# Encoder block on one core: another order of loads, norm sums and head rotations ahead of attention

## The chip, the core and the metric

The kernel runs on one core of a Trainium2 chip. The core has a matrix engine (PE, with its weight load shown apart as PEld), a vector engine (DVE), a scalar engine (ACT), a general engine (POOL), and a queue of its own for transfers (SP, "SPq" in the rows). The metric is the device time of one execution in microseconds (us); less is better.

## The reference

One layer of an encoder over 1024 tokens of width 1024, in float32:

```
mod = silu(c) @ ada_w + ada_b                    # six vectors of 1024: sh1, sc1, g1, sh2, sc2, g2
h   = rmsnorm(x, norm1_w) * (1 + sc1) + sh1
proj = h @ w_in                                  # q 512 | k 128 | v 128 | z 1024 | xbc 1536 | dt 32 | gates 2048
q, k = axial_rope(rmsnorm(q, q_gain)), axial_rope(rmsnorm(k, k_gain))      # per head of 64
att  = softmax(q k^T / 8) v                      # 8 heads, 2 key/value heads
ssd  = rmsnorm((scan forward + scan backward) * silu(z))                   # state space branch on conv(xbc)
x    = x + g1 * ((gate0 * (att @ w_attn_up) + gate1 * (ssd @ w_ssd_up)) @ w_out)
h2   = rmsnorm(x, norm2_w) * (1 + sc2) + sh2
x    = x + g2 * peer(h2)                         # 8 heads, top 16 of 16384 experts per head
out  = rmsnorm(x, final_norm_w)
```

Only the lines down to `q, k` are touched by the change.

## The kernel before

Everything is held transposed: features stand on the 128 partitions, tokens run along the free axis, so `x` is eight parts of 128 x 1024. Products keep float32 precision by splitting both operands into a high and a low half; `mm3` (L203 to L207) issues three matmuls of 128x512 for each pair, high-high, high-low, low-high. A half is made by `split`: ACT rounds to the high half (L175), another engine subtracts (L176). `w_in` is cut into 43 output tiles of 128; one tile is 8 parts x 2 token halves x 3 = 48 matmuls. `weights` loads a tile in two pieces (`wr`), casts them on ACT (`wh`) and subtracts on POOL (`wl`); each of these names has 3 or 4 buffers.

Two stages matter here.

**First norm (pool `p0`, to L309).** `shift_scale(m)` forms one column each of shift and scale: 128 rows of `ada_w` are loaded (`at`), multiplied by silu(c) with a running sum on DVE (L254), the bias is added (L255), and the scale is joined with the norm's weight (L271). Beside that, ACT squares the eight parts of `x` (L282), PE sums the squares over partitions (`sums`, L212), `rstd` takes the reciprocal root on DVE and ACT with two Newton steps (L218 to L224), PE spreads the result over partitions (`rbcast`, L233) and ACT copies it out (`rb`, L293). Then each part of `x` is multiplied by `rb` (L296), scaled and shifted on ACT (L299), split into `hh` and `hl`, and taken at once into three output tiles, `FIRST = (4, 0, 1)`: keys, and the first two query tiles. The order in DVE, POOL and ACT is that of the code (`manual`).

**Heads (pool `pr`, to L404).** Five tiles hold keys (4) and queries (0 to 3), two heads in each; further tiles made in this stage are values (5) and two gate tiles. For each of the five: `norms` squares the tile, sums over each head's 64 partitions and calls `rstd`; `heads` spreads it (`rbcast`), multiplies with gain (L358), swaps halves of 32 partitions (L360), multiplies by sine on DVE (L362) and by cosine on POOL (L361), adds (L363) and writes high halves (ACT, L368 to L376) and low halves (DVE, L369 to L378). In this stage a scheduler of the program's builder sets the order within each engine. After it comes attention, whose first work on DVE is the row maximum (L450), interleaved with the convolution tiles of the state space branch on PE.

The later stages take the same instructions in both kernels, and each engine has them in the same order from the second of the 16 attention steps on.

Of the kernel before, what the change touches and what calls it, by code (L numbers as in the profile page):

```python
# [20 lines left out]
D = 1024  # L21
# [48 lines left out]
K_BSEL, K_QSEL, N_KN, K_HSEL, K_U, K_L, K_GT, K_LT, N_KB = 0, 32, 544, 544, 1568, 1696, 1824, 1952, 2080  # L70
# [10 lines left out]
def constants():  # L81
# [6 lines left out]
    ka[p, K_FOLD + p % 64] = 1.0  # L88
    kb = np.zeros((128, N_KB), np.float32)
    kb[p, K_BSEL + p // 64] = 1.0  # L90
# [3 lines left out]
    for i in range(4):  # L94
        for s in range(2):
            kb[32 * i + s, K_QSEL + 128 * i + 64 * s:K_QSEL + 128 * i + 64 * s + 64] = 1.0
# [7 lines left out]
    return {"ka": ka, "kb": kb, "kr": kr}  # L104
# [16 lines left out]
def block(ctx, tc, A, out, dbg=None):  # L121
# [143 lines left out]
    done = manual("DVE", "Pool", "Activation")  # L265
    cs = condition(p0.tile([128, D], F32, name="cs"))

    def shift_scale(m):
        ada(m, m + 1, at_tile, cs)
        ada(8 + m, 9 + m, at_tile, cs)  # L270
        V.scalar_tensor_tensor(A1[:, m:m + 1], mod[:, 8 + m:9 + m], 1.0, cols[:, C_N1 + m:C_N1 + m + 1], op0=OP.add, op1=OP.mult)  # L271
# [12 lines left out]
    raws = [p0.tile([128, 8, 128], F32, name="w3r", bufs=2) for _ in range(2)]  # L284
    for m, raw in zip(FIRST[1:], raws):
        nc.sync.dma_start(raw, A["wi"][m])
# [53 lines left out]
    def norms(m, raw):  # L340
        sq = pr.tile([128, S], F32, name="sq")
        ACT.activation(sq, raw, AF.Square)
        acc = P1()
        sums(sq, acc, S, True, True, kb[:, K_BSEL:K_BSEL + 32])
        return m, raw, rstd(pr, acc, S, 1.0 / 64, 3)
# [9 lines left out]
    def heads(m, raw, r):  # L355
        rb = rbcast(P2(), r, S, kb[:, K_QSEL:K_QSEL + 512])
        g = cols[:, C_KG:C_KG + 1] if m == 4 else cols[:, C_QG:C_QG + 1]
        V.scalar_tensor_tensor(v2(raw), v2(raw), g, rb, op0=OP.mult, op1=OP.mult)  # L358
        sw = pr.tile([128, S], F32, name="sw")
        V.stream_shuffle(sw, raw, list(range(16, 32)) + list(range(16)))  # L360
        POOL.tensor_tensor(raw, raw, cos, op=OP.mult)  # L361
        V.tensor_tensor(sw, sw, sin, op=OP.mult)  # L362
        V.tensor_tensor(raw, raw, sw, op=OP.add)  # L363
        dump("qk", m, raw)
        a, b = raw[0:64], raw[64:128]
        if m < 4:
            e, f = qs[2 * m], qs[2 * m + 1]
            ACT.copy(e[0:64], a)  # L368
# [1408 lines left out]
```

## Time and profile before

| | us |
|---|---|
| median of 3 runs (lowest, highest) | 4008.17 (4002.51, 4011.59) |
| the profiled execution, its own time | 4000.45 |
| its span in the profile | 3998.6 |
| PE busy in the span | 3633.1 (91%) |
| DVE, POOL, ACT busy | 2601.3, 1828.6, 1357.6 |

Shares of busy time are means over stages with different limits. The profile's second part shows PE busy for about 5 and 7 tenths in the first two of 40 slices of 100 us and 9 or more tenths in nearly all that follow, with a granted clock of 0.8 of full speed in the first slice. The rows of this stage are in the section on the rows below.

### The profile page before, as it was taken

The page shows a single profiled execution, that of the slowest core. Times are in us where ns is not written, and L with a number is a line of the kernel's source. Part 1 is how long each engine was busy: PE and PEld are TensorE (multiplying, and loading weights), DVE is VectorE, ACT ScalarE, POOL GpSimd, SP SyncE. Part 2 cuts the span into 40 slices and gives each one's busy share as a digit, 9 for nine tenths or more (in the row PEclk, how much of TensorE's full clock was granted, in tenths as well). Part 3 has the DMA queues.
Part 4 walks back from the last instruction along what each step waited for, and adds up shares of the span by engine and source line. Part 5 has one row for each costly group of instructions (what it writes and reads, how often), then busy time and mean ns, then how long its engine had stood idle before and what let it go on. Part 6 is the DMA issues. An engine that isn't in the chain of part 4 may idle for free. (4 is left out here: it accounts for less than half of the span.)

```text
span 3998.6 us, 61125 instructions
## 1 busy us (share of the span) xinstructions
PE 3633.1 (91%) x22927; PEld 3188.4 (80%) x22927; DVE 2601.3 (65%) x5316; ACT 1357.6 (34%) x2658; POOL 1828.6 (46%) x1529
## 2 busy tenths in 40 slices
PE   5799999998898899998888889699999999999998
PEld 3577777776687889996768789697888999788897
DVE  5688851356673578877785467684457898544556
ACT  4265542223333433332226555322222222222222
POOL 3211113555455557777875466444443444444200
PEclk8899999998899999999999899799999999999999
DMA  5111124323366349897777678888887898888732
GB/s 184 37 47 43 54 89 141 103 92 120 96 219 192 119 135 327 310 320 232 248 256 258 226 265 330 326 297 316 317 317 256 299 293 295 300 312 310 246 115 81
DMA packets 386920, 852.08 MB, mean 213 GB/s; under 512 B 32704, under 2 KB 146880, under 8 KB 383808
## 3 DMA queue, kind: packets, MB, share of 16 engines
q1 hardware_dynamic: 276032, 445.47, 33.1%
q0 software_dynamic: 110592, 402.70, 28.8%
q8 instruction: 180, 2.95, 0.3%
q14 instruction: 116, 0.95, 0.1%
HBM read 739.45 MB, written 108.59 MB: 212 GB/s over the span
## 5 line engine op out<-in xcount | busy, mean ns | idle before, releaser
L205 PE MATMUL hb<-ah,wh 128*128 128x320 f32 x2048 | 653.4, 319 | 25.5 <-ACT a L1369 25.5
L207 PE MATMUL hb<-ah,wl 128*128 128x320 f32 x2048 | 641.0, 313 | 9.6 <-issue 9.6
L206 PE MATMUL hb<-al,wh 128*128 128x320 f32 x2048 | 640.1, 313 | 0.0
L1192 POOL DMA_INDIRECT br<-u,bidx x384 | 373.0, 971 | 364.0 <-DVE br L1224 235.4
L195 POOL TENSOR_TENSOR wl<-wr,wh 128x512 fp32r<-128x512 f32 x269 | 352.5, 1316 | 394.6 <-ACT wh L194 364.6
L205 PE MATMUL pb<-Wh,vh 128*128 128x320 f32 x1536 | 476.8, 317 | 55.6 <-ACT Wh L1599 31.7
L176 POOL TENSOR_TENSOR wl<-wr,wh 128x512 fp32r<-128x512 f32 x170 | 232.1, 1369 | 634.9 <-ACT wh L175 455.6
L1192 POOL DMA_INDIRECT br<-v,ixt x384 | 380.0, 990 | 268.4 <-PE gx L1271 154.1
L206 PE MATMUL pb<-Wl,vh 128*128 128x320 f32 x1536 | 480.6, 313 | 2.1 <-DVE Wl L1602 2.1
L207 PE MATMUL pb<-Wh,vl 128*128 128x320 f32 x1536 | 478.7, 312 | 0.6 <-issue 0.6
L1224 DVE SCALAR_TENSOR_TENSOR br<-br,gx 128x1024 f32<-128x1024 f32 x384 | 454.0, 1215 | 8.0 <-DMA br<-u,bidx 5.4
L205 PEld LDWEIGHTS hb<-ah,wh 128*128 128x128 f32 x2048 | 392.5, 192 | 55.2 <-ACT a L1369 29.9
L207 PEld LDWEIGHTS hb<-ah,wl 128*128 128x128 f32 x2048 | 391.5, 191 | 11.0 <-issue 10.9
L206 PEld LDWEIGHTS hb<-al,wh 128*128 128x128 f32 x2048 | 391.9, 191 | 0.0
L1632 DVE TENSOR_TENSOR acc<-acc,pb 128x320 f32<-128x320 f32 x491 | 230.3, 485 | 231.2 <-PE pb L207 170.6
L175 ACT CAST vh<-vr 128x512 fp32r<-128x512 f32 x256 | 151.8, 619 | 636.2 <-PE pb L206 415.5
L205 PEld LDWEIGHTS pb<-Wh,vh 128*128 128x128 f32 x1536 | 289.7, 190 | 84.1 <-ACT Wh L1599 34.9
L194 ACT CAST wh<-wr 128x512 fp32r<-128x512 f32 x288 | 178.3, 619 | 402.5 <-PE hb L206 144.3
L206 PEld LDWEIGHTS pb<-Wl,vh 128*128 128x128 f32 x1536 | 292.4, 190 | 6.3 <-DVE Wl L1602 4.7
L207 PEld LDWEIGHTS pb<-Wh,vl 128*128 128x128 f32 x1536 | 292.6, 190 | 0.4
L1388 DVE TENSOR_TENSOR quad<-io,rig 128x1024 f32<-128x1024 f32 x160 | 191.6, 1221 | 136.7 <-PE pb L1403 77.1
L176 DVE TENSOR_TENSOR vl<-vr,vh 128x512 fp32r<-128x512 f32 x256 | 198.5, 776 | 80.9 <-ACT vh L175 70.0
(362 smaller groups left out, 8266.9 us busy)
## 6 DMA issues: line engine op xcount, KB each, us to landing
wr<-uT SPq DMA_DIRECT2D x256, 256.0 KB
vr<-v SPq DMA_DIRECT2D x256, 256.0 KB
G_d<-stg SPq DMA_DIRECT2D x20, 2048.0 KB
gt<-G_d SPq DMA_DIRECT2D x42, 960.0 KB
a_d<-a SPq DMA_DIRECT2D x85, 320.0 KB
a<-a_d SPq DMA_DIRECT2D x85, 320.0 KB
wr<-wi SPq DMA_DIRECT2D x82, 256.0 KB
sq<-adaT SPq DMA_DIRECT2D x32, 512.0 KB
```

Of the source, the lines that this page charges most:

```text
L175: ACT.copy(hi, src)
L176: (eng or POOL).tensor_tensor(lo, src, f32(hi), op=OP.subtract)
L194: ACT.copy(h, raw)
L195: late.append(lambda: (eng or POOL).tensor_tensor(w, raw, f32(h), op=OP.subtract))
L205: PE.matmul(o, lhsT=wh, rhs=xh, start=first, stop=False)
L206: PE.matmul(o, lhsT=wh, rhs=xl, start=False, stop=False)
L207: PE.matmul(o, lhsT=wl, rhs=xh, start=False, stop=last)
L1192: POOL.indirect_dma_start(out=r, out_offset=None, in_=A[tab], in_offset=bass.IndirectOffsetOnAxis(ap=idx, axis=0))
L1224: V.scalar_tensor_tensor(v2(r), v2(r), 1.0, hrow[0], op0=OP.mult, op1=OP.mult, accum_out=a[:, s:s + 1])
L1388: V.tensor_tensor(x, iota.unsqueeze(1).unsqueeze(1).to_broadcast([128, 2, 4, 128]), ig[:, 0:2, t:t + 4].unsqueeze(3).to_broadcast([128, 2, ...
L1632: V.tensor_tensor(acc[:, m, js], acc[:, m, js], o, op=OP.add)
```

## The change

In the first norm:
- The parts of `x` are loaded ahead of the rows of `ada_w`; the vector silu(c) is written to PSUM (`csP`) and read from there by the projections' products (L285 of the changed kernel, L254 before).
- The running sums go to `sums1`; bias and norm weight are folded in by one tiny ACT instruction for each column (L290, L294) in place of L255 and L271. The first scale column is formed before `rstd`, the other three of the first four after it.
- The spread `rstd` stays in PSUM (`rb`, two banks); multiplication by it and by the scale is one DVE instruction for each token half (L322). ACT adds the shift alone, and POOL makes the low halves `hl` of the first seven parts (DVE before).
- `FIRST` is two tiles, (4, 0); tile 1 is made in the head stage. PE's order is written by hand here too.

In the head stage:
- The norms are batched: one `rstd` for tiles 4 and 0, one for 1 and 2, one for 3. The selecting matrices for this are wider (constant `kb`, 1572 columns where 544 were loaded here).
- The product with cosine moves from POOL to DVE.
- The order on PE and DVE is written by hand: half tiles of projections on PE stand between the spreads and sums, and each rotation (`rotate`, `highs`, `lows`) has its place among them.

The diff, without the layout of constants and the helper functions that keep their text:

```diff
-    for m in range(2):
-        shift_scale(m)
+    done = manual("DVE", "Pool", "Activation", "PE")
+    FIRST = (4, 0)
     xt = p0.tile([128, 8, S], F32, name="xt")
+    cs = p0.tile([128, D], F32, name="cs")
+    nc.sync.dma_start(cs, A["cv"].to_broadcast([128, D]))
     for m in range(8):
         nc.sync.dma_start(xt[:, m], A["xT"][:, m])
-    FIRST = (4, 0, 1)
+    csP = P2()
+    ACT.activation(csP, v2(cs), AF.Silu)
+    def project(i):
+        at = at_tile()
+        nc.sync.dma_start(at, A["adaT"][i])
+        V.scalar_tensor_tensor(v2(at), v2(at), 1.0, csP, op0=OP.mult, op1=OP.mult, accum_out=sums1[:, i:i + 1])
+    def scale_of(m):
+        project(8 + m)
+        n1 = cols[:, C_N1 + m:C_N1 + m + 1]
+        ACT.activation(A1[:, m:m + 1], sums1[:, 8 + m:9 + m], AF.Identity, bias=pre[:, m:m + 1], scale=n1)
...
+    scale_of(0)
     r = rstd(p0, acc, S, 1.0 / D)
-    W3 = [weights(A["wi"][FIRST[0]], 8)]
-    for raw in raws:
-        W3.append([p0.tile([128, 8, 128], FR, name=n, bufs=2) for n in ("w3h", "w3l")])
-        split(raw, *W3[-1])
-    rb = p0.tile([128, S], F32, name="rb")
-    ACT.copy(v2(rb), rbcast(P2(), r, S))
+    shift_of(0)
+    scale_of(1)
+    shift_of(1)
+    raw = p0.tile([128, 8, 128], F32, name="w3r")
+    nc.sync.dma_start(raw, A["wi"][FIRST[0]])
+    W3 = [[p0.tile([128, 8, 128], FR, name=n) for n in ("w3h", "w3l")]]
+    split(raw, *W3[0])
+    W3.append(weights(A["wi"][FIRST[1]], 8))
+    rb = [P1() for _ in range(2)]
...
     for m in range(8):
-        (POOL if m > 1 else V).tensor_tensor(xt[:, m], xt[:, m], rb, op=OP.mult)
-    for m in range(8):
-        t = xt[:, m]
-        ACT.activation(t, t, AF.Identity, bias=mod[:, m:m + 1], scale=A1[:, m:m + 1])
-        split(t, hh[:, m], hl[:, m], V)
+        x = xt[:, m]
+        for j, o in enumerate(rb):
+            js = slice(512 * j, 512 * j + 512)
+            V.scalar_tensor_tensor(x[:, js], x[:, js], A1[:, m:m + 1], o, op0=OP.mult, op1=OP.mult)
+        if m < 7:
+            ACT.activation(x, x, AF.Identity, bias=mod[:, m:m + 1], scale=1.0)
+            split(x, hh[:, m], hl[:, m])
+        else:
+            ACT.activation(hh[:, m], x, AF.Identity, bias=mod[:, m:m + 1], scale=1.0)
+            V.scalar_tensor_tensor(hl[:, m], x, mod[:, m:m + 1], f32(hh[:, m]), op0=OP.add, op1=OP.subtract)
...
         if m < 6:
-            shift_scale(m + 2)
+            scale_of(m + 2)
+            shift_of(m + 2)
...
-        POOL.tensor_tensor(raw, raw, cos, op=OP.mult)
-        V.tensor_tensor(sw, sw, sin, op=OP.mult)
+            V.tensor_tensor(sw, sw, sin, op=OP.mult)
+            V.tensor_tensor(raw, raw, cos, op=OP.mult)
...
+    done = manual("PE", "DVE")
...
+    raws[1], go = tile_of(1)
+    next(go)
+    k_, q0 = normed_heads(4, 0)
+    next(go)
+    ra, ha, la = turned(*k_)
+    raws[2], go = tile_of(2)
+    next(go)
+    ra()
+    ha()
+    rb_, hb, lb = turned(*q0)
+    next(go)
+    la()
+    raws[3], go = tile_of(3)
+    next(go)
+    rb_()
+    hb()
+    q1, q2 = normed_heads(1, 2)
+    lb()
+    next(go)
+    ra, ha, la = turned(*q1)
+    go = gate_of(24 - NGQ)
+    next(go)
+    ra()
+    ha()
+    rb_, hb, lb = turned(*q2)
+    next(go, None)
+    la()
+    q3, = normed_heads(3)
+    go = gate_of(25 - NGQ)
+    next(go)
+    rb_()
+    hb()
+    ra, ha, la = turned(*q3)
+    next(go, None)
+    lb()
+    last, go = tile_of(5)
+    next(go)
+    ra()
+    ha()
+    next(go)
+    la()
+    values_of(last)
```

Where the change moves instructions, the order of three places shows it. First the transfer queue SP from the start of the program. Before:

```order
L138 DMA ka<-ka 128x832
L140 DMA cols<-cols 128x162
L142 DMA rows<-rows 128x64
L258 DMA cs<-cv 128x1024
L253 DMA at<-adaT 128x1024 x4
L277 DMA xt<-xT 128x1024 x8
L286 DMA w3r<-wi 128x1024 x2
L186 DMA wr<-wi 128x512 x2
L253 DMA at<-adaT 128x1024 x8
L186 DMA wr<-wi 128x512 x3
```

and in the changed kernel:

```order
L142 DMA ka<-ka 128x832
L144 DMA cols<-cols 128x162
L146 DMA rows<-rows 128x64
L273 DMA cs<-cv 128x1024
L275 DMA xt<-xT 128x1024 x8
L284 DMA at<-adaT 128x1024 x4
L307 DMA w3r<-wi 128x1024
L190 DMA wr<-wi 128x512 x2
L284 DMA at<-adaT 128x1024 x12
L190 DMA wr<-wi 128x512 x6
L356 DMA kb<-kb 128x1572
```

The eight parts of `x` stand ahead of the first four `at`, and `kb` stands behind six weight pieces.

Second POOL, whose `wl` and `w3l` are low halves of weights, in the first norm. Before:

```order
L176 TENSOR_TENSOR wl<-wr,wh 128x512 x2
L176 TENSOR_TENSOR w3l<-w3r,w3h 128x1024 x2
L296 TENSOR_TENSOR xt<-xt,rb 128x1024 x6
L176 TENSOR_TENSOR wl<-wr,wh 128x512 x8
L361 TENSOR_TENSOR raw<-raw,cos 128x1024
```

and in the changed kernel:

```order
L180 TENSOR_TENSOR w3l<-w3r,w3h 128x1024
L180 TENSOR_TENSOR wl<-wr,wh 128x512 x2
L180 TENSOR_TENSOR hl<-xt,hh 128x1024 x4
L180 TENSOR_TENSOR wl<-wr,wh 128x512 x2
L180 TENSOR_TENSOR hl<-xt,hh 128x1024
L180 TENSOR_TENSOR wl<-wr,wh 128x512
L180 TENSOR_TENSOR hl<-xt,hh 128x1024 x2
L180 TENSOR_TENSOR wl<-wr,wh 128x512 x13
```

POOL loses six products with `rb` and the products with cosine, and gains seven low halves of `x`, with three weight pieces among them.

Third DVE at the end of the head stage, where `qs` are the low halves of queries, `rstd` with larger numbers belongs to the last tile normed, `vs` to the values, and `st` is the first work of attention. Before:

```order
L371 TENSOR_TENSOR qs_460<-raw,qs_460 64x1024
L222 TENSOR_TENSOR rstd_256_954<-rstd_256_953 128x256
L223 SCALAR_TENSOR_TENSOR rstd_256_954<-rstd_256_954,rstd_256_952 128x256
L224 SCALAR_TENSOR_TENSOR rstd_256_953<-rstd_256_954,rstd_256_953 128x256
L358 SCALAR_TENSOR_TENSOR raw<-raw,cols,pa 128x1024
L360 STREAM_SHUFFLE sw<-raw 128x1024
L362 TENSOR_TENSOR sw<-sw,sin 128x1024
L363 TENSOR_TENSOR raw<-raw,sw 128x1024
L369 TENSOR_TENSOR qs_461<-raw,qs_461 64x1024
L371 TENSOR_TENSOR qs_462<-raw,qs_462 64x1024
L413 TENSOR_SCALAR half<-cols 128x12
L450 TENSOR_REDUCE st<-s 128x1 x2
```

and in the changed kernel:

```order
L414 TENSOR_TENSOR qs_406<-raw,qs_406 64x1024
L415 TENSOR_TENSOR qs_407<-raw,qs_407 64x1024
L392 SCALAR_TENSOR_TENSOR raw<-raw,cols,pa 128x1024
L394 STREAM_SHUFFLE sw<-raw 128x1024
L395 TENSOR_TENSOR sw<-sw,sin 128x1024
L396 TENSOR_TENSOR raw<-raw,cos 128x1024
L397 TENSOR_TENSOR raw<-raw,sw 128x1024
L414 TENSOR_TENSOR qs_408<-raw,qs_408 64x1024
L415 TENSOR_TENSOR qs_409<-raw,qs_409 64x1024
L503 TENSOR_SCALAR half<-cols 128x12
L385 TENSOR_TENSOR vs<-pa,vs 128x16x64
L540 TENSOR_REDUCE st<-s 128x1 x2
```

The last `rstd` no longer ends between two rotations but stands a whole rotation earlier, and the low half of the values is the last instruction before attention.

## Rows read from the trace of the kernel before

**Rows 1.** Windows: stretch, length, busy us and count by engine, granted clock, DMA share, GB/s

```profile
174.00:206.00 32.00, 13.10 (x45) 10.04 (x46) 24.30 (x26) 6.85 (x7) 5.99 (x4) 0.68 0.00 0
...
240.00:263.00 23.00, 23.00 (x117) 18.41 (x115) 20.84 (x33) 14.97 (x25) 4.13 (x5) 1.00 0.16 52
```

**Rows 2.** PE's waits from 0 to 206 us: total us, times, longest

```profile
PE pa L233 <- DVE rstd L224: 31.7, 3, 18.5
...
PE pa L206 <- DVE hl L176: 8.7, 3, 5.4
```

**Rows 3.** Timeline of DVE, first row maximum of attention

```profile
205.71 2.35 DVE L450 TENSOR_REDUCE st<-s 128x1 f32<-128x1024 f32 x2
```

**Rows 4.** Timeline, loads and first rstd: start, duration, engine, line, operation, [idle before]

```profile
10.15 1.23 DVE L254 SCALAR_TENSOR_TENSOR at<-at,cs 128x1024 f32<-128x1024 f32 x1 [10.15 <-DMA at<-adaT]
...
20.39 1.06 ACT L282 ACTIVATE sq<-xt 128x1024 f32<-128x1024 f32 x1 [0.21 <-DMA xt<-xT]
...
24.24 1.06 ACT L282 ACTIVATE sq<-xt 128x1024 f32<-128x1024 f32 x1 [0.22 <-DMA xt<-xT]
25.32 1.28 ACT L219 ACT_TABLE_LOAD   x1
...
27.06 1.75 DVE L220 RECIPROCAL rstd<-rstd 128x256 f32<-128x256 f32 x1 [0.58 <-ACT rstd L219]
...
30.73 5.00 POOL L176 TENSOR_TENSOR w3l<-w3r,w3h 128x1024 fp32r<-128x1024 f32 x2
...
36.04 0.42 DVE L223 SCALAR_TENSOR_TENSOR rstd<-rstd,rstd 128x256 f32<-128x256 f32 x1
36.49 0.42 DVE L224 SCALAR_TENSOR_TENSOR rstd<-rstd,rstd 128x256 f32<-128x256 f32 x1
...
36.97 3.78 PE L233 MATMUL pa<-rstd,ka 128*128 128x256 f32 x8 [10.98 <-DVE rstd L224]
```

**Rows 5.** Timeline of the loop over eight parts in the first norm, DVE

```profile
49.57 3.38 DVE L254 SCALAR_TENSOR_TENSOR at<-at,cs 128x1024 f32<-128x1024 f32 x1
...
67.95 1.22 DVE L254 SCALAR_TENSOR_TENSOR at<-at,cs 128x1024 f32<-128x1024 f32 x1
...
69.22 0.16 DVE L255 TENSOR_TENSOR mod<-mod,cols 128x1 f32<-128x1 f32 x1
```

**Rows 6.** The same loop, ACT

```profile
71.00 1.25 ACT L299 ACTIVATE xt<-xt,mod,A 128x1024 f32<-128x1024 f32 x1 [1.68 <-DVE A L271]
72.28 1.05 ACT L175 CAST hh<-xt 128x1024 fp32r<-128x1024 f32 x1
```

**Rows 7.** Line L941 on DVE: ns least, median, most; first and last start

```profile
L941 DVE SCALAR_TENSOR_TENSOR t<-bh,A,pb x8: 604/612/615, 1276.2 to 1302.3; 128x384 f32<-128x384 f32 x8
```

**Rows 8.** Timeline of POOL in the stretch of that line

```profile
1301.44 1.27 POOL L176 TENSOR_TENSOR wl<-wr,wh 128x512 fp32r<-128x512 f32 x1 [0.47 <-ACT wh L175]
```

**Rows 9.** Groups of DVE by shape, 0 to 210 us: busy, mean ns, idle before

```profile
L362 DVE TENSOR_TENSOR sw<-sw,sin 128x1024 f32<-128x1024 f32 x5 | 10.3, 2070 | 0.1
...
L358 DVE SCALAR_TENSOR_TENSOR raw<-raw,cols,pa 128x1024 f32<-128x1024 f32 x5 | 6.4, 1276 | 15.8 <-PE pa L233 15.8
```

**Rows 10.** Timeline of PE, projections, sums and spreads

```profile
62.63 0.63 PE L207 MATMUL pa<-hh,wl 128*128 128x512 f32 x1
...
65.62 0.56 PE L205 MATMUL pa<-hh,w3h 128*128 128x512 f32 x1
...
77.41 0.40 PE L207 MATMUL pa<-hh,wl 128*128 128x512 f32 x1
...
91.41 0.40 PE L207 MATMUL pa<-hh,w3l 128*128 128x512 f32 x1
...
99.44 0.64 PE L212 MATMUL pb<-sq,kb 128*32 128x256 f32 x8
...
141.22 1.89 PE L233 MATMUL pa<-rstd,kb 128*128 128x256 f32 x8
...
190.78 3.75 PE L233 MATMUL pa<-rstd,kb 128*128 128x256 f32 x8 [18.48 <-DVE rstd L224]
```

More of the change, by code (lines that the diff above doesn't have):

```diff
@@ L338, in raw_tile, with norms @@
         return raw
-    def norms(m, raw):
-        sq = pr.tile([128, S], F32, name="sq")
-        ACT.activation(sq, raw, AF.Square)
+    def norms(tiles):
         acc = P1()
-        sums(sq, acc, S, True, True, kb[:, K_BSEL:K_BSEL + 32])
-        return m, raw, rstd(pr, acc, S, 1.0 / 64, 3)
+        for n, (_, raw) in enumerate(tiles):
+            sq = pr.tile([128, S], F32, name="sq", bufs=2)
+            ACT.activation(sq, raw, AF.Square)
+            at = K_BSEL + 4 - 2 * n
+            sums(sq, acc, S, n == 0, n == len(tiles) - 1, kb[:, at:at + 32])
+        r = rstd(pr, acc, S, 1.0 / 64, 2)
+        return [(m, raw, r, n) for n, (m, raw) in enumerate(tiles)]
     def values_of(raw):
@@ L380, in block @@
-    raws = []
-    for m, o in zip(FIRST, O3):
-        raw = pr.tile([128, S], F32, name="raw", bufs=5)
-        ACT.copy(v2(raw), o)
-        raws.append((m, raw))
-    raws.append((2, raw_tile(2)))
-    ready = [norms(*r) for r in raws[:3]]
-    raws.append((3, raw_tile(3)))
-    heads(*ready[0])
-    for m in range(24 - NGQ, 24):
-        t = pr.tile([128, S], F32, name="sq")
-        o = P2()
-        for j, oj in w_in(19 + m, lambda j: o[:, j]):
-            ACT.copy(t[:, j * 512:(j + 1) * 512], oj)
-        nc.sync.dma_start(g_d[m - 8], t)
@@ L395, in block, with turned, rotate, highs @@
-    heads(*ready[1])
-    ready.append(norms(*raws[3]))
-    last = raw_tile(5)
-    heads(*ready[2])
-    heads(*ready[3])
-    ready = norms(*raws[4])
+    def turned(m, raw, r, n):
+        rb = rbcast(P2(), r, S, kb[:, K_QSEL + 512 * n:K_QSEL + 512 * n + 512])
+        def rotate():
+            g = cols[:, C_KG:C_KG + 1] if m == 4 else cols[:, C_QG:C_QG + 1]
+            V.scalar_tensor_tensor(v2(raw), v2(raw), g, rb, op0=OP.mult, op1=OP.mult)
+            sw = pr.tile([128, S], F32, name="sw")
+            V.stream_shuffle(sw, raw, list(range(16, 32)) + list(range(16)))
+            V.tensor_tensor(sw, sw, sin, op=OP.mult)
+            V.tensor_tensor(raw, raw, cos, op=OP.mult)
+            V.tensor_tensor(raw, raw, sw, op=OP.add)
+            dump("qk", m, raw)
+        def highs():
+            a, b = raw[0:64], raw[64:128]
+            if m < 4:
+                ACT.copy(qs[2 * m][0:64], a)
+                ACT.copy(qs[2 * m + 1][64:128], b)
+            else:
+                for g, src in ((0, a), (1, b)):
+                    for s in range(2):
+                        ACT.copy(kh[g][s * 64:s * 64 + 64], src)
+        def lows():
+            a, b = raw[0:64], raw[64:128]
+            if m < 4:
+                e, f = qs[2 * m], qs[2 * m + 1]
+                V.tensor_tensor(e[64:128], a, f32(e)[0:64], op=OP.subtract)
+                V.tensor_tensor(f[0:64], b, f32(f)[64:128], op=OP.subtract)
+            else:
+                for g, src in ((0, a), (1, b)):
+                    own = f32(kh[g])[g * 64:g * 64 + 64]
+                    for s in range(2):
+                        V.tensor_tensor(kl[g][s * 64:s * 64 + 64], src, own, op=OP.subtract)
+        return rotate, highs, lows
@@ new lines, in tile_of, with steps, normed_heads @@
+    def tile_of(m, name="raw", bufs=5):
+        t = pr.tile([128, S], F32, name=name, bufs=bufs)
+        o = P2()
+        def steps():
+            for j, oj in w_in(m, lambda j: o[:, j]):
+                ACT.copy(t[:, j * 512:(j + 1) * 512], oj)
+                yield
+        return t, steps()
+    raws = {}
+    for m, o in zip(FIRST, O3):
+        raws[m] = pr.tile([128, S], F32, name="raw", bufs=5)
+        ACT.copy(v2(raws[m]), o)
+    done = manual("PE", "DVE")
+    def normed_heads(*ms):
+        return norms([(m, raws[m]) for m in ms])
@@ new lines, in gate_of @@
+    def gate_of(m):
+        t, go = tile_of(19 + m, "sq", 2)
+        next(go)
+        yield
+        next(go)
+        nc.sync.dma_start(g_d[m - 8], t)
+    raws[1], go = tile_of(1)
[16 more added lines that the diff above has]
+    lb()
@@ L401, in block @@
+    next(go)
[16 more added lines that the diff above has]
+    last, go = tile_of(5)
+    next(go)
+    ra()
+    ha()
+    next(go)
+    la()
     values_of(last)
-    heads(*ready)
+    done()
     pr.release()
```

60 lines of the change are left out of this document (22 added, 38 removed).

## The prediction

> **What bounds the kernel now.** I read the busy shares by slice first, then the windows of the first 263 us, then who PE waits for, then the timeline from 0 to 206 us engine by engine. Attention leaves PE no slack: in its second step PE is busy for 23.00 of 23.00 us at full clock, with DVE at 20.84 [rows 1]. So before attention the question is only when PE may begin it. In the last stretch of the heads, 174 to 206 us, PE works for 13.10 of 32.00 us at a granted clock of 0.68, while DVE is busy for 24.30 [rows 1]. Over the first 206 us PE's largest wait in the heads is for the Newton steps of `rstd`: 31.7 us in three waits, the longest 18.5 [rows 2]; that longest one lies where the last head's sum is spread at 190.78 [rows 10], because DVE's order puts its three last Newton instructions behind two other rotations. In the loop over the eight parts PE waits 8.7 us for DVE's low halves [rows 2]. Attention's first instruction on DVE starts at 205.71 [rows 3]. That start is what the change moves; the queues behind it are in the same order from attention's second step on, so I carry its shift to the end of the program undiminished.
>
> **Loads and first rstd.** Before, the ninth transfer of 512 KB, counted from the one that lands at 10.15, releases the square at 20.39, and three further ones take to 24.24, 1.28 each [rows 4]. After, `x` takes places one to eight, so its last part lands at 19.1 and its square and sums are done by 21.3. The ninth is the row for the first scale column, at 20.4. Its product on DVE took 1.22 from SBUF, 1.27 with what follows [rows 5]. With silu(c) in PSUM no such product is in the trace with a running sum; the nearest rows, 1.22 [rows 5] and 1.28 for the gain product that reads PSUM [rows 9], bound it, also from below. I take 1.28, so 21.7. The ACT instruction on one column is not in the trace either: between nothing and the 0.42 of a 128x256 instruction on DVE [rows 4]; I take 0.25, so 21.9. Now the table load of 1.28, which ran beside the sums before [rows 4], stands in line: 23.2. Root 0.42, reciprocal 1.75, six Newton instructions at 0.45 from start to start [rows 4]: 28.2. Before it was 36.9, because POOL ran its two large subtractions of 5.00 us through the Newton steps [rows 4]; after, POOL's first subtraction stands behind them. The spread takes 3.78 [rows 4], and three more projections of 1.28 hide it: DVE begins on the parts at 32.1.
>
> **The loop.** ACT's two columns, then the cast of the key weights (1.05, by the cast of rows 6), end at 33.4. POOL then has one subtraction of 128x1024 (half of 5.00, 2.5 [rows 4]), two of 128x512 (1.30 each by the row of 1.27 [rows 8]) and the first low half of `x` (2.5): 41.1, and PE can run. From there each part costs DVE two half products and two projections. A half product of 512 columns: 0.61 at 384 [rows 7] and 1.28 at 1024 [rows 9] give 0.74, or 0.67 from start to start, an estimate; so 2 x 0.67 + 2 x 1.28 = 3.9. These have at most one operand in SBUF. A projection of two took 3.38 beside POOL in place of 1.22 [rows 5]; the half products with a PSUM operand at L941 took 0.615 at most, the last of them within a subtraction of POOL [rows 7, 8], so I stretch nothing here. ACT needs 1.25 + 1.05 [rows 6] and two columns, 2.8. POOL needs 2.5. PE needs 12 matmuls. Its two rates are 60 matmuls from 77.41 to 91.41, 0.233 each at 2.4 GHz, and 7 from 62.63 to 65.62, 0.427 each at 1.2 GHz, after a wait; it had changed to the faster level some 4 us after it resumed [rows 10]. So 5.1 for the first part and 2.8 for the later ones. PE's first four parts end near 54.6. In ACT's new order a cast for the third projection's weights stands ahead of the sixth shift and needs a buffer that PE frees there. So shift and cast of the sixth part end at 57.5, POOL follows at 60.0 and 62.8, and DVE's low half of the eighth at 64.0; three parts of 2.8 on PE from 60.0 end at 68.4. That is with two projections done, not three.
>
> **The heads.** Six tiles of 48 matmuls: 67.2. Five sums of 0.6 and five spreads of 1.9 [rows 10]: 12.5. Eight transposes, at most one spread: 1.6. Each `rstd` takes 0.42 + 0.42 + 1.75 + 2.7 and handovers, 5.6; half a tile, 24 matmuls, covers 5.6. The first meets POOL's weight pieces (1.5 late). The second is queued on DVE behind a whole rotation (five instructions of 1.2 to 1.3, 6.2) and begins 0.6 late and meets POOL again: 2.5. The third is even. So 4.0 of waits: 68.4 + 67.2 + 12.5 + 1.6 + 4.0 = 153.7. The values' cast and low half, 1.0 and 1.2 by the same shapes in rows 6 and 5, end at 155.9, where DVE comes free as well: its last rotation starts near 142. So attention starts 205.71 - 155.9 = 49.8 earlier.
>
> **Given back.** Before, while DVE finished, PE had already run 44 matmuls of the first convolution tile between the second and third pair of score products; in the new order 20 stand there. PE owes 24 x 0.233 = 5.6 in a stage without slack. Gain 49.8 - 5.6 = 44. The `kb` load is 805 KB behind six weight pieces and needs the space of `x`, free at 64; at 1.28 per 512 KB it lands by 68, and the first sums need it at 74. If that cover went, each us late costs one.
>
> The profiled execution took 4000.45, its span 3998.6, so 1.8 lie around it. 4000.45 - 44 = 3956.5. The median of the runs shown is 7.7 above that execution; I take the median as base: 4008 - 44 = 3964.
>
> **Rivals.**
> - *DVE falls behind in the heads.* Each rotation gets a third instruction with both inputs in SBUF, the cosine product, and POOL still has 13 weight pieces of 1.3 there. The sine products, with POOL's cosine beside them, took 2.07 in the mean [rows 9], against 1.22 for such a shape alone [rows 5]. If every piece blocks DVE for its length, that is 17 us, of which I counted 3: gain 44 - 14 = 30, 3978. The Trainium skill (SBUF — State Buffer, Who interferes with whom) states that: a DVE instruction with two SBUF inputs contends with a GpSimd instruction that reads SBUF, and the loser is blocked until the other ends. By that rule this rival's 17 would be due where all pieces meet such an instruction; the trace agrees on the blocking and leaves open how many meet. Against it: POOL no longer holds cosine products, and ACT's casts place the pieces near the ends of PE's tiles.
> - *Nothing of the pacing binds.* If PE runs on from 41.1 at one slow part and seven fast ones it ends the loop at 65.8, the `rstd` waits go to 0.5, and the debt of 5.6 is absorbed in attention's first step: gain 44 + 2.6 + 3.5 + 5.6 = 56, 3952.
> - *The clock falls: slower than before.* The new PE order has short waits all through, in the loop (2.8 of work in every 3.9) and before each spread. At 1.2 GHz throughout, 96 + 288 matmuls cost 0.194 more each, less the 2.3 counted: 72; sums, spreads and transposes 13 more (a spread takes 3.75 there, 1.89 at 2.4 GHz [rows 10]); the waits of 6 vanish under it. 79 - 44 = 35 slower, 4043. It decides once the slow level holds for over half of the 112 us from 41 on. Against it: after its wait of 5.4 us [rows 2] PE came back to the fast level in some 4 us and then kept it over the 60 matmuls [rows 10]; the slow level in 174 to 206 us goes with a PE idle for most of it [rows 1]. The Trainium skill (TensorE: Matmul & The Clock Gate, A second HAM failure mode) describes a kernel in which short idle stretches between groups of matmuls let the clock swing between the levels. By that rule this rival would hold in part; no row here has short waits of that kind over a long stretch.
> - *The gain is lost later.* A transfer-bound stage downstream would absorb the earlier start: within 8 of before, 4004. PE's 9 tenths nearly everywhere after the first 200 us speak against it.
>
> **How the numbers follow.** My forecast 0.65, DVE behind 0.15, no pacing 0.12, clock 0.04, lost later 0.04. The forecast's own range adds the unknown prices: columns on ACT 4 x 0.2, projections 0.2, POOL's 2.5 stretched as the projection of rows 5 was, by at most 0.9 a part on seven parts, 6, all on the late side; on the early side the debt of 5.6; and 4 for the spread of a median, the runs shown reaching from 4002.51 to 4011.59: 3954 to 3976. The range of 8 in 10 takes in most of the two neighbours with the same spread of 4 (3952 - 4, 3978 + 4 and half of the columns and ports above): 3948 to 3986. A change of under 0.2%, 8 us, can't be told from none here. Only the last rival lands in it, 0.04, and only the clock gives slower, 0.04; faster 0.92.
>
> **What would show it.** In the profile after: first `rstd` done near 28 with no stretched Newton steps; PE's first projection run near 41 and the end of the two at 68; no PE wait of over 3 us in the heads; the first row maximum near 156; from there the same durations. A granted clock near 0.7 from 41 to 150, or waits of PE for DVE of over 10 us in all in the heads, would make it wrong, as would a shift that shrinks between attention and the end.

## The result, and the profile after

The changed kernel takes 3962.69 us in the median of four runs (3956.84 to 3964.8), the kernel before, run beside it, 4009.88: a ratio of 0.9895, 95% interval 0.9878 to 0.9912. Run again later the ratio was 0.9911 (0.9895 to 0.9926). The forecast was 3964. So the gain is 47.2 us between the first pair of medians and 35.3 between the second (4001.47 and 3966.18); 44 were forecast.

The profiled execution of the changed kernel took 3962.2, its span 3960.4 (3998.6 before). The first thing to read is where its attention begins. Timeline of DVE, the first row maximum, which answers to [rows 3]:

```profile
157.18 1.22 DVE L540 TENSOR_REDUCE st<-s 128x1 f32<-128x1024 f32 x1
```

That is 48.5 us earlier, where 49.8 were forecast. PE's waits from 0 to 206 us (in all, times, longest), which answer to [rows 2]:

```profile
PE pb L216 <- ACT sq L299: 12.7, 8, 11.2
PE pb L315 <- DVE rstd L228: 7.1, 1, 7.1
PE pa L210 <- POOL hl L180: 4.5, 3, 3.3
PE pa L237 <- DVE rstd L228: 4.2, 2, 3.3
PE pa L209 <- ACT hh L179: 4.1, 1, 4.1
PE s L537 <- DVE vs L385: 1.4, 1, 1.4
```

No wait in the heads is left near the 18.5 of before: the spreads (L237) wait 4.2 in all. The longest stand before PE has a projection with a low half to do, which is at 40.36. Windows of the same kernel (length, busy us and count by engine, granted clock, DMA share, GB/s), which answer to [rows 1]:

```profile
70.00:100.00 30.00, 29.15 (x143) 22.57 (x145) 22.36 (x23) 12.62 (x18) 7.38 (x5) 1.00 0.15 44
100.00:130.00 30.00, 26.68 (x121) 20.42 (x110) 19.74 (x22) 10.09 (x15) 5.41 (x4) 0.89 0.10 38
130.00:157.00 27.00, 24.65 (x109) 19.19 (x107) 22.54 (x25) 9.94 (x13) 6.36 (x6) 1.00 0.21 68
180.00:203.00 23.00, 22.69 (x112) 17.67 (x111) 20.93 (x33) 14.20 (x23) 2.71 (x4) 1.00 0.16 52
```

PE is busy for some 0.9 or more of each stretch shown; one of them, 100 to 130, has a clock below 1.00, which the working did not have.

The first norm, timeline, answering to [rows 4] (loads and first `rstd`), and then PE up to its first projection:

```profile
20.44 1.22 DVE L285 SCALAR_TENSOR_TENSOR at<-at,pa 128x1024 f32<-128x1024 f32 x1 [16.03 <-DMA at<-adaT]
...
21.70 0.39 ACT L290 ACTIVATE A<-sums,pre,cols 128x1 f32<-128x1 f32 x1 [1.48 <-DVE at L285]
22.10 1.28 ACT L223 ACT_TABLE_LOAD   x1
...
23.85 1.75 DVE L224 RECIPROCAL rstd<-rstd 128x256 f32<-128x256 f32 x1 [1.84 <-ACT rstd L223]
...
27.93 0.43 DVE L228 SCALAR_TENSOR_TENSOR rstd<-rstd,rstd 128x256 f32<-128x256 f32 x1
```

```profile
28.41 3.78 PE L315 MATMUL pb<-rstd,ka 128*128 128x256 f32 x8 [7.05 <-DVE rstd L228]
36.26 0.79 PE L209 MATMUL pa<-hh,w3h 128*128 128x512 f32 x1 [4.07 <-ACT hh L179]
40.36 0.80 PE L210 MATMUL pa<-hl,w3h 128*128 128x512 f32 x1 [3.30 <-POOL hl L180]
```

The groups of DVE from 0 to 70 us (mean ns after the busy time), answering to [rows 5]:

```profile
L285 DVE SCALAR_TENSOR_TENSOR at<-at,pa 128x1024 f32<-128x1024 f32 x16 | 18.9, 1220 | 16.0 <-DMA at<-adaT 16.0
L322 DVE SCALAR_TENSOR_TENSOR xt<-xt,A,pb 128x512 f32<-128x512 f32 x16 | 11.3, 747 | 1.3 <-ACT A L290 1.3
```

No projection is stretched: 16 of them take 1.22 in the mean, POOL at work beside them or not. Then the heads on PE, answering to [rows 10]:

```profile
79.20 1.97 PE L237 MATMUL pa<-rstd,kb 128*128 128x256 f32 x8 [0.85 <-DVE rstd L228]
...
109.80 3.78 PE L237 MATMUL pa<-rstd,kb 128*128 128x256 f32 x8 [3.32 <-DVE rstd L228]
...
113.02 0.99 PE L209 MATMUL pa<-hh,wh 128*128 128x512 f32 x1
...
119.91 1.89 PE L237 MATMUL pa<-rstd,kb 128*128 128x256 f32 x8
...
121.44 0.59 PE L209 MATMUL pa<-hh,wh 128*128 128x512 f32 x1
...
133.60 1.96 PE L237 MATMUL pa<-rstd,kb 128*128 128x256 f32 x8
```

Four of the five spreads run at 2.4 GHz. The third begins after a wait of 3.32 and takes 3.78, as long as the one of before that ran at 1.2 GHz (3.75 in [rows 10]), and the matmul behind it 0.99 instead of 0.59. What the wait was for stands on ACT and DVE:

```profile
101.70 1.05 ACT L403 CAST qs<-raw 64x1024 fp32r<-64x1024 f32 x1 [1.40 <-DVE raw L397]
102.77 1.04 ACT L404 CAST qs<-raw 64x1024 fp32r<-64x1024 f32 x1
103.84 0.42 ACT L223 ACTIVATE rstd<-rstd 128x256 f32<-128x256 f32 x1
```

```profile
101.58 0.42 DVE L222 TENSOR_SCALAR rstd<-pb 128x256 f32<-128x256 f32 x1
104.29 1.75 DVE L224 RECIPROCAL rstd<-rstd 128x256 f32<-128x256 f32 x1 [2.29 <-ACT rstd L223]
```

The root of tiles 1 and 2 could start at 102.0; ACT has two casts of tile 0's query ahead of it, so DVE waits 2.29.

Last, what comes after attention's start. The row maxima from first to last start, before and then after:

```profile
L450 DVE TENSOR_REDUCE st<-s x64: 1205/1216/1226, 205.7 to 549.2; 128x1 f32<-128x1024 f32 x64
```

```profile
L540 DVE TENSOR_REDUCE st<-s x64: 1203/1214/1225, 157.2 to 506.5; 128x1 f32<-128x1024 f32 x64
```

The lead of 48.5 is 42.7 at the last of them: 5.8 were given back within attention. Nearly all of it goes at one place. The fourth row maximum comes 48.2 earlier than before (214.20 before), the fifth 42.4 (217.15 before):

```profile
166.00 1.22 DVE L540 TENSOR_REDUCE st<-s 128x1 f32<-128x1024 f32 x1
...
174.78 1.21 DVE L540 TENSOR_REDUCE st<-s 128x1 f32<-128x1024 f32 x1
```

Between the two PE runs 24 matmuls of the convolution tile in one piece, from 166.61 to 172.3. Lines of the state space stage up to 1119 us in the profile of before keep 42.5 to 42.7. In the expert stages the lead is 38 to 42 in most lines, 33.0 at the last start of one (3426.4 before, 3393.4 after), and 38.2 at the end of these two executions. Single executions of one kernel lie up to 18 us (changed) and 29 us (before) apart, so two profiles can't tell what the expert stages keep.

### The profile page after: what moved, and what is told of

The parts are those of the page before. It is cut to its first block, busy times and chain, and to the rows that moved or that the text cites. A ratio compares the mean times of both kernels' runs of the same rounds, so it can differ in the third digit from the quotient of the medians.

```text
span 3960.4 us, 61117 instructions
## 1 busy us (share of the span) xinstructions
PE 3631.6 (92%) x22927; PEld 3189.8 (81%) x22927; DVE 2574.5 (65%) x5289; ACT 1356.3 (34%) x2672; POOL 1803.3 (46%) x1526
## 5 line engine op out<-in xcount | busy, mean ns | idle before, releaser
L209 PEld LDWEIGHTS hb<-ah,wh 128*128 128x128 f32 x2048 | 391.9, 191 | 52.7 <-ACT a L1459 28.2
L211 PEld LDWEIGHTS hb<-ah,wl 128*128 128x128 f32 x2048 | 390.7, 191 | 11.3 <-POOL wl L199 10.3
```

The source lines that it names most:

```text
L209: PE.matmul(o, lhsT=wh, rhs=xh, start=first, stop=False)
L211: PE.matmul(o, lhsT=wl, rhs=xh, start=False, stop=last)
```

## The experiments

All are edits of the changed kernel; two of them put back a whole half of the kernel before. They are read by the start of attention's first row maximum, since the whole time of one run scatters by some 10 us or more:

| kernel | attention at | us, runs |
|---|---|---|
| before | 205.71 | 4009.88, 4 |
| changed kernel | 157.18; again 157.48 | 3962.69, 4; again 3966.18, 6 |
| silu(c) in SBUF | 166.34 | 3973.11, 1 |
| first rows ahead of `x` | 160.77 | 3967.09, 1 |
| cosine product on POOL | 168.56 | 3984.63, 1 |
| low halves of `x` on DVE | 179.41 | 3990.25, 1 |
| new norm, old heads | 191.13 | 3981.04, 1 |
| old norm, new heads | 178.48 | 3978.31, 1 |
| heads' order left to the scheduler | 163.93 | 3968.03, 1 |
| root ahead of the casts | 154.43 | 3955.68, 1 |
| spread behind the half tile | 156.92 | 3955.69, 1 |
| both of these and earlier weight casts (`b2`) | 155.14 | 3957.74, 4 |
| root and earlier weight casts (`b3`) | 153.49 | 3958.4, 6 |

This reading has a scatter of its own. In the kernels whose edit lies behind it the first norm's spread begins between 28.41 and 29.27, and from that spread to the heads' first sums the changed kernel took 43.1 in one profile and 44.2 in the other. Differences near 1 us are not read from the table.

### Where silu(c) stands

```diff
-    csP = P2()
-    ACT.activation(csP, v2(cs), AF.Silu)
+    ACT.activation(cs, cs, AF.Silu)
+    csP = v2(cs)
```

> The changed kernel, but silu(c) stays in SBUF instead of a PSUM tile, so that each product of a row of the modulation matrix (L285) reads two SBUF tiles. Read by the profile: the start of attention (its first row maximum), 157.2 us in the changed kernel, and the time of one L285, 1.22 us there. Theory A (two SBUF operands on VectorE stand against GpSimd's subtractions of 2.4 us each): L285 goes to up to 3.6 us in the loop, a part's 3.6 us on VectorE to as much as 6.0 in six parts, and attention starts 3 to 14 us later (160 to 171), less what TensorE had in hand. Theory B (the PSUM place buys nothing): L285 stays within 0.05 us of 1.22 and attention starts at 157.2 within 0.5.

Attention starts 9.2 later. Groups of DVE from 0 to 70 us, and one projection in the loop:

```profile
L285 DVE SCALAR_TENSOR_TENSOR at<-at,cs 128x1024 f32<-128x1024 f32 x16 | 29.9, 1907 | 16.2 <-DMA at<-adaT 16.2
```

```profile
34.32 3.37 DVE L285 SCALAR_TENSOR_TENSOR at<-at,cs 128x1024 f32<-128x1024 f32 x1
```

Theory A holds. The mean goes from 1.22 to 1.91, single ones from 1.22 to 3.43, and PE's wait for `hl` from 4.5 to 11.3. POOL loses too: five of its seven low halves of `x` take 3.1 to 3.4, all of them 2.4 in the changed kernel. The product itself is no faster from PSUM (1.22 in either place while POOL is idle); what PSUM buys is that POOL doesn't meet it. The Trainium skill (SBUF — State Buffer, Who interferes with whom) says that of a DVE instruction with two SBUF inputs and a GpSimd instruction that reads SBUF the one that comes second is blocked; this trace agrees: the product above starts at 34.32, while a subtraction of POOL runs from 33.28 to 36.60, and ends only at 37.69.

### The order of the loads

The first four rows of `ada_w` are loaded ahead of `x`:

```diff
+    early = {}
+    for i in (8, 0, 9, 1):
+        early[i] = p0.tile([128, D], F32, name="at", bufs=NAT)
+        nc.sync.dma_start(early[i], A["adaT"][i])
     for m in range(8):
         nc.sync.dma_start(xt[:, m], A["xT"][:, m])
```

> The changed kernel, but the first four rows of the modulation matrix (8, 0, 9, 1) are loaded ahead of the input instead of behind it. Theory A (the input's loads set the first root): four rows of 512 KB at 1.28 us a piece put the first Square from 10.1 to about 15.2 us and the last from 19.2 to 24.3; the first product no longer stands between the sums and the root, which takes back about 1.2; the root comes 3.5 to 5 us later and attention starts 2 to 5 us later (159 to 162), the lower end if the weights' casts and GpSimd's chain have slack. Theory B (the end of the first norm is set by the loads of weights and rows, whatever the order): attention starts at 157.2 within 1.

Attention starts 3.6 later. The first spread begins at 31.20 instead of 28.41 and PE's first low half comes at 44.40 instead of 40.36. That is the middle of theory A's range, with a root 2.8 later where it had put 3.5 to 5. Of the 8.6 us by which the change brought the spread forward (36.97 in [rows 4]), the order of the loads makes 2.8. Most of the rest lies between reciprocal and spread, 9.9 before and 4.6 after, where POOL's subtractions stood beside the Newton steps: four of the six took 0.79 to 2.44 before, and all six take 0.42 or 0.43 after.

### The cosine product

```diff
-            V.tensor_tensor(sw, sw, sin, op=OP.mult)
-            V.tensor_tensor(raw, raw, cos, op=OP.mult)
+            POOL.tensor_tensor(raw, raw, cos, op=OP.mult)
+            V.tensor_tensor(sw, sw, sin, op=OP.mult)
```

> The changed kernel, but in the rotation of a head tile the product with the cosines is back on GpSimd, beside VectorE's product with the sines. Theory A (the prediction's: VectorE has room in the heads, so its move there bought little by itself): GpSimd's product takes 2.4 us beside VectorE's two, each of five rotations ends 1 to 2.4 us later, and attention starts 0 to 3 us later (157 to 160), since TensorE waits for a root and not for a rotation. Theory B (the rotation is on the path that sets the end of the heads): five times 1.2 to 2.4, attention 6 to 12 us later (163 to 169). VectorE's shuffle or sine product should stretch from 1.2 to over 2 us where GpSimd is at work beside it.

Attention starts 11.4 later: theory B, near its upper end, and a miss of the one I held. A group of DVE and one of POOL in the heads, and PE's largest wait there:

```profile
L397 DVE TENSOR_TENSOR raw<-raw,sw 128x1024 f32<-128x1024 f32 x5 | 7.2, 1440 | 11.4 <-POOL raw L395 11.4
L395 POOL TENSOR_TENSOR raw<-raw,cos 128x1024 f32<-128x1024 f32 x5 | 17.1, 3416 | 16.7 <-DVE sw L394 12.8 <-issue 3.9
```

```profile
PE pa L209 <- ACT raw L430: 7.0, 3, 4.5
```

The sum of the rotation waits for POOL's product, 2.3 each time. That makes ACT's casts of the tile late, and behind them in ACT's queue stand the copies (L430) that free PE's accumulators. PE's waits for these copies are 11.8 in all, 7.0 of them in the line above, against 1.2 in the changed kernel; those for roots are 0.9. So what PE newly waits for is neither a root nor a rotation, but a copy queued behind a cast that waits for a rotation. My theory A had looked only at what PE waits for now.

I had also expected the product on DVE to stretch. It did not: the sine product took 1.225. POOL's did, 3.42 in the mean. Which of the two is lengthened goes by which starts first. In all five rotations here DVE's starts first, by 0.10 or less. The kernel before has both orders; here POOL starts first:

```profile
169.02 2.35 POOL L361 TENSOR_TENSOR raw<-raw,cos 128x1024 f32<-128x1024 f32 x1 [3.13 <-DVE sw L360]
169.14 3.31 DVE L362 TENSOR_TENSOR sw<-sw,sin 128x1024 f32<-128x1024 f32 x1
```

In two of its rotations POOL's product comes first and takes 2.35 and 2.42, DVE's 3.31 and 3.36; in the other three DVE's comes first and takes 1.23, POOL's 3.43 or 3.44. So about 1.0 of the 2.3 in each rotation is POOL's product standing behind DVE's, and the rest is that it is the slower of the two by itself.

### Low halves of x on DVE

```diff
-            split(x, hh[:, m], hl[:, m])
+            split(x, hh[:, m], hl[:, m], V)
```

> The changed kernel, but the low halves of the normalized input (seven of eight parts) are made by VectorE instead of GpSimd. Theory A (the prediction's: VectorE's 3.6 us a part is the pace of the loop): a part goes to 4.8 (a subtraction of 1.2) or 6.0 (of 2.4 as the one of part 7), the last part comes 7 to 17 us later, TensorE ends the two projections at 72 to 82 instead of 67, and attention starts 5 to 14 us later (162 to 171); TensorE's first matmul with a low half comes earlier, near 37.5 instead of 40.4. Theory B (GpSimd's 2.4 us a part is the pace or its queue is, as TensorE waits for it first): with GpSimd free the loop is no longer and attention starts at 157 or up to 3 us earlier.

Attention starts 22.2 later, more than either theory. Two starts of the low half, one part apart:

```profile
44.41 1.22 DVE L180 TENSOR_TENSOR hl<-xt,hh 128x1024 fp32r<-128x1024 f32 x1 [2.29 <-ACT hh L179]
...
51.53 1.23 DVE L180 TENSOR_TENSOR hl<-xt,hh 128x1024 fp32r<-128x1024 f32 x1 [2.29 <-ACT hh L179]
```

A part now costs 7.1 on DVE: 3.6 as before, 1.2 for the subtraction, and 2.3 in which DVE waits for ACT's shift and cast of the same part, with its next products queued behind. DVE's work sets the pace, as theory A has it, but the price is the round trip through ACT. POOL was not a spare hand for 1.2 us of work; it took a wait out of DVE's queue.

### The two halves of the change

The first kernel keeps the new loads and first norm and has the head stage of before; the second has the first norm of before, with two tiles beside it, and the new head stage:

```diff
-    k_, q0 = normed_heads(4, 0)
...
+    raws.append((1, raw_tile(1)))
+    raws.append((2, raw_tile(2)))
+    ready = [norms(*r) for r in raws[:3]]
```

```diff
-    rb = [P1() for _ in range(2)]
...
+    rb = p0.tile([128, S], F32, name="rb")
+    ACT.copy(v2(rb), rbcast(P2(), r, S))
...
+        (POOL if m > 1 else V).tensor_tensor(xt[:, m], xt[:, m], rb, op=OP.mult)
```

> The changed kernel's loads and first norm, with two tiles beside it, and behind them the head stage as it stood before (each tile's root by itself, the order left to the scheduler, the cosine product on GpSimd); tile 1 is projected at the head of that stage instead of beside the norm. Attention's first row maximum: 205.7 us before, 157.2 in the changed kernel. Theory A (the two halves of the change add up: the norm is worth about 26 of the 48.5 us, the heads about 22): 177 to 183 here, and TensorE's wait of 18.5 us for a root is still there. Theory B (the wait for the root is a matter of how late the third tile was, so the norm alone mends it): below 172, and no wait of TensorE over 6 us in the heads.

> The kernel before up to the end of its first norm, but with two tiles (4 and 0) beside the norm instead of three, and behind it the changed head stage. Theory A (the halves add up): attention starts at 180 to 187, TensorE's waits for roots in the heads are 4 to 6 us in all. Theory B (the new head stage gains only because it starts early): 190 or later. The sum of the two gains, this one's and that of the kernel with the norm alone, is 48.5 within 4 by A.

With the norm alone attention is 14.6 earlier than before, with the heads alone 27.2. Theory A gave 177 to 183 and 180 to 187 and missed both, and the sum is 41.8, outside 48.5 within 4. The halves are not cut cleanly: both kernels have two tiles beside the norm, and the second kernel's norm spread comes at 33.87 already, where it was 36.97 before. PE's timeline with the norm alone, then with the heads alone:

```profile
176.40 3.54 PE L237 MATMUL pa<-rstd,kb 128*128 128x256 f32 x8 [20.13 <-DVE rstd L228]
```

```profile
94.67 1.94 PE L216 MATMUL pb<-sq,kb 128*32 128x256 f32 x16 [6.14 <-DMA kb<-kb]
```

With the old head stage the long wait stays, at 20.1 after 18.5 before: theory B of the first kernel falls. With the old norm, PE waits 6.14 for the constant `kb`, whose load is issued at 88.22; PE's waits for roots in the heads are 3.5 in all. In the changed kernel the load is issued at 61.93, when the last reader of `x` ends (DVE, L328). With the old norm the last reader of `x` ends at 84.5, but ahead of `kb` in the transfer queue stands a weight piece, issued at 87.84, when POOL's subtraction that frees its buffer ends (86.53 to 87.81); that subtraction waited for ACT's cast, and the cast until 85.77 for PE. By its size this wait is the part of the gain that only both halves together have, 14.6 + 27.2 + 6.1 = 47.9; no run takes it away alone, so that is argued and not shown.

### The hand-kept order of the heads

```diff
-    done = manual("PE", "DVE")
+    done = lambda: None
```

> The changed kernel, but the order of TensorE's and VectorE's instructions in the head stage is left to the scheduler instead of being kept as the code has it. What the scheduler lays down differs at few places: on TensorE the last spread of a root stands 15 matmuls later, on ScalarE the casts of two query tiles and the copies of gate tiles change places. Theory A (the hand-kept order is what removes the wait of 18.5 us): attention starts at 165 or later. Theory B (the wait goes because the code asks for the norms of two tiles at once and a half tile ahead, and the scheduler would do as well): 155 to 159.

Attention starts 6.8 later, between the two theories. PE's longest wait for a root is 2.7 (5.3 in three), so the long one does not come back; PE's waits for ACT's copies grow from 0.7 to 4.0. So the wait of 18.5 went with the code's own order and its joint norms; which of the two did it no run separates. Keeping that order by hand is worth 6.8, or 4.8 counted from the heads' first spread (81.13 here, 79.20 there).

### The root ahead of the casts

```diff
+    act = manual("Activation")
     rb_()
-    hb()
     q1, q2 = normed_heads(1, 2)
+    hb()
+    act()
     lb()
```

> The changed kernel, but on ScalarE the square root of tiles 1 and 2 stands ahead of the two casts of tile 0's query (1.05 us each) instead of behind them. In the changed kernel VectorE waits 2.29 us for that root, TensorE then 3.32 us for the spread, and its eight spread matmuls take 3.78 us instead of 1.89, with slow ones behind them until 115.3. Theory A: the root comes 1.8 us earlier and TensorE waits 1.5; if the clock then holds, attention starts 1.8 + 1.9 + 1.2 = up to 4.9 us earlier (152.3); if it falls all the same, 1.8 earlier (155.4). Theory B (VectorE's subtractions of tile 0, late by the casts, or the end of the rotations set the start of attention): 157.2 within 0.5.

Attention starts 2.8 earlier. ACT, then PE:

```profile
102.61 0.42 ACT L223 ACTIVATE rstd<-rstd 128x256 f32<-128x256 f32 x1 [1.69 <-DVE rstd L222]
```

```profile
109.71 1.99 PE L237 MATMUL pa<-rstd,kb 128*128 128x256 f32 x8 [2.62 <-DVE rstd L228]
...
117.14 1.89 PE L237 MATMUL pa<-rstd,kb 128*128 128x256 f32 x8
```

The clock holds (granted 1.00 in 106 to 111 and in 111 to 116, against 0.76 and 0.56 in the changed kernel), and the next spread comes 7.43 later instead of 10.11: the clock had cost 2.7. The wait fell by 0.7 alone, since two Newton steps on DVE now lasted 1.4 and 1.6. Against the first spread (79.81 here, 79.20 there) attention gains 3.4, which is 2.7 + 0.7; against the changed kernel's second profile, whose clock cost 1.7, it gains 2.3 (80.52 to 157.48 there). Theory A in kind; its upper figure had counted a wait of 1.5.

### The spread behind the half tile

```diff
-    ra, ha, la = turned(*q1)
     go = gate_of(24 - NGQ)
     next(go)
+    ra, ha, la = turned(*q1)
     ra()
```

> The changed kernel, but the eight matmuls that spread the root of tile 1 stand behind the first half of the next gate tile (24 matmuls, 5.6 us) instead of ahead of it; nothing else on TensorE or VectorE is moved (on ScalarE two weight casts change places). In the changed kernel TensorE waits 3.32 us there, and runs at 1.2 GHz up to 115.3. Theory A: the half tile covers the wait, the clock holds, TensorE has 3.3 + 3.0 = 6.3 us less to do; VectorE takes up tile 1 at 113.6 as now and has 8.5 us of waits behind it to give, so attention starts 4 to 6.3 us earlier (151 to 153). Theory B (VectorE's chain of four rotations from tile 1 on sets the start): less than 2 us earlier.

Attention starts 0.3 earlier, or 1.0 counted from the heads' first spread (79.98 here). Counted so, it starts 76.94 after the spread, and 76.96 in the changed kernel's second profile: theory B, and no gain shown. The wait was moved, not removed. PE, the fifth spread and the first scores:

```profile
131.09 1.97 PE L237 MATMUL pa<-rstd,kb 128*128 128x256 f32 x8 [2.81 <-DVE rstd L228]
```

```profile
154.81 0.79 PE L537 MATMUL s<-kh,qs 128*128 128x512 f32 x1 [2.36 <-DVE vs L385]
155.40 0.63 PE L537 MATMUL s<-kl,qs 128*128 128x512 f32 x1
```

DVE takes up tile 1 no earlier (114.62 for 113.62), so the last root is now late (2.81, none before), and the scores wait 2.36 instead of 1.43 and run at 1.2 GHz (0.63 each).

### Versions meant to be faster

`b2` has the two edits above and a third; `b3` has the root and the third alone. The third casts the first norm's weights earlier:

```diff
     shift_of(0)
-    scale_of(1)
-    shift_of(1)
     raw = p0.tile([128, 8, 128], F32, name="w3r")
...
     W3.append(weights(A["wi"][FIRST[1]], 8))
+    scale_of(1)
+    shift_of(1)
```

> The changed kernel with three edits: the root of tiles 1 and 2 ahead of the query casts on ScalarE, the spread of tile 1 behind the half tile, and the casts of the first norm's weights ahead of the second pair of columns on ScalarE (L179 from 32.0 to about 30, so that GpSimd's first product with a low half comes up to 1.7 us earlier). Expected: attention starts at 149.5 to 153, against 154.4 with the root alone and 157.2 in the changed kernel; the weights' casts add 0 to 1.2 of it, since TensorE's later waits in the norm (0.3 and 0.9 us) take the rest back. The whole kernel: 3954 to 3960 us, 0.999 of the changed kernel's time.

> The changed kernel itself, for comparison in the same call: 3957 to 3965 us, attention's first row maximum at 157.2 within 0.5, TensorE's wait of 3.3 us at the spread of tile 1 and the clock below full speed there again.

> The changed kernel with the two edits that the runs bore out: the root of tiles 1 and 2 ahead of the query casts on ScalarE, and the casts of the first norm's weights ahead of the second pair of columns; the spread of tile 1 stays where the changed kernel has it. Expected: the head stage's first sums on TensorE 0.7 to 0.8 us earlier after the first spread than with the root alone (72.09 there, its first spread at 29.27; 71.34 with all three edits, at 29.26), attention's first row maximum at 153.7 (154.43 with the root alone, 157.2 to 157.5 in the changed kernel), no fall of the clock at the spread of tile 1. The whole kernel: 3953 to 3962 us, 3 to 5 us below the changed kernel, which its scatter of some 10 us hardly shows. A rival: the earlier start only lengthens TensorE's next wait in the first norm, and attention starts at 154.4.

Ratios to before: `b2` 0.9893 (0.9878 to 0.9907), the changed kernel on the same chip 0.9911 (0.9895 to 0.9926), its median a little above the 3965 expected; `b3`, on another, 0.9891 (0.9874 to 0.9907). `b2` misses its range for attention's start by 2.1: what the late spread does was seen above. In the profile the two edits are 3.7 to 4.0 earlier where attention starts; in the whole time the intervals overlap, so no gain over the changed kernel is shown. PE's first projection with a low half in `b3`, and its later wait:

```profile
38.67 0.79 PE L210 MATMUL pa<-hl,w3h 128*128 128x512 f32 x1 [1.88 <-POOL hl L180]
54.26 0.50 PE L210 MATMUL pa<-hl,w3h 128*128 128x512 f32 x1 [1.83 <-POOL hl L180]
```

PE starts 1.7 earlier and waits 1.8 at 54 (0.3 and 0.9 before). The heads' first sums come 42.1 after the norm's spread, 42.8 with the root alone: 0.7 is kept.

## Why the prediction was right

- **Loads and first rstd: right.** Done at 28.36, forecast 28.2. The unknown prices were near: the column on ACT 0.39 for 0.25, the product from PSUM 1.22 for 1.28.
- **The loop: right in time, but it held more work.** A part took DVE 3.60 (3.9), PE's first low half came at 40.36 (41.1), the eighth part's at 61.9 (64.0), the two projections ended at 67.7 (68.4). From 36 to 67.6 PE ran 104 matmuls, where the two projections have 96: eight of tile 1's, 1.9 us, already stand in PE's waits there. The forecast says "with two projections done, not three" and left all 48 to the heads, so by the work done its loop was 2.6 too long and not 0.7. That products with one input in PSUM are not stretched was argued from L941; the kernel with silu(c) in SBUF shows it, and that 9.2 us hung on it. The eighth low half, with both inputs in SBUF, was stretched: 2.49 beside POOL's last subtraction, and 1.28 where POOL makes none (low halves on DVE).
- **The heads: right in sum by luck, wrong in its terms.** The waits for roots were 4.2 for 4.0, as 0.85, 3.32 and 0 for 1.5, 2.5 and 0. The step "it begins 0.6 late and meets POOL again: 2.5" left out what stands ahead of the root on ACT: two casts, 1.8. It came near only because POOL was priced too high: DVE began 0.9 late, and one Newton step took 1.37 for 0.42. Of the signs to look for, "no PE wait of over 3 us in the heads" failed. And the sum priced all five spreads at 2.4 GHz, while the third and the matmuls behind it ran at 1.2: 2.7. Two short waits for ACT's copies, 0.67 and 0.56, were not in the working; the second fell within the 1.6 put for the transposes. What covered these was not foreseen either: the eight matmuls already done, 1.9, and a spread's price. From 119.91 to 121.44 one holds PE for 1.5, and the matmul behind it costs 0.2 more than a usual one; I had put 1.9, so five of them are some 0.7 too much.
- **Attention's start:** 157.18 for 155.9, from errors in both directions.
- **Given back: right, mechanism included.** 5.8 for 5.6, between the fourth and the fifth row maximum, where PE runs 24 matmuls of the convolution tile, the number forecast.
- **Carried to the end: right to 1119 us, open behind it.** The lead stays at 42.5 to 42.7 through the state space stage. What the later stages do to it (33 to 42 in these two profiles; medians 47.2 and 35.3 apart) can't be told from their scatter with these runs. By its own execution the forecast was 3956.5, and the profiled one took 3962.2.
- **The rivals.** DVE did not fall behind: its sine products took 1.226 in the mean. But the cosine product was more than a load that DVE could bear, as the prediction treated it: put back on POOL, it costs 11.4. The clock rival was right about the mechanism at one place, a wait before a spread, for 2.7 us where it had counted 85.

## What to carry to other kernels

Before moving an instruction between engines, list what is queued behind it and behind each instruction that waits for it: both surprises here, the cosine product (11.4 us for five products of 1.2) and the low halves (22.2 us for seven of 1.2), were round trips between in-order queues more than work; in the cosine's case about 1.0 of each 2.3 was POOL's product waiting out DVE's. Where a VectorE product with two SBUF inputs ran beside a busy GpSimd, moving one input to PSUM was worth 9.2 us for two changed lines. A wait moved off its place is only gone if the engine that was late gets its input earlier; the spread put half a tile later came back as two waits.

## What the runs showed of the hardware that was not expected

The clock after a short wait of PE is not settled by the wait's length. After 3.32 it was at 1.2 GHz from the first spread matmul on, and cost 2.7; in the second profile of the same kernel, after 3.29, the eight took 3.59 and the next spread came 9.10 later instead of 7.43, a cost of 1.7. After 2.62, 2.63 and 2.81 it held, and after 3.28 too, in the kernel with the old norm and the new heads (its spread took 1.99). After 2.36 in front of the scores it had fallen in one kernel (0.63 a matmul, above) and held in another whose order there is the same; `b2`:

```profile
153.91 0.50 PE L539 MATMUL s<-kh,qs 128*128 128x512 f32 x1 [2.36 <-DVE vs L385]
154.24 0.39 PE L539 MATMUL s<-kl,qs 128*128 128x512 f32 x1
```

What decides it, these runs do not tell. These readings go by durations, because the granted clock of a row doesn't always agree with them: from 28.40 to 32.20 in the changed kernel it is given as 1.00, and the eight matmuls of the first spread there take 3.78.

The second thing is how even the blocking between DVE and POOL is. In the ten pairs of a sine product on DVE and a cosine product on POOL in two kernels, both with two inputs in SBUF, the one that started first took its usual time (1.2 on DVE, 2.4 on POOL), and the other about as much longer as the first still had to run (3.4 on POOL, 3.3 to 3.4 on DVE); a start that the profile puts 0.04 ahead was enough.
